# Weight sums formed at four places of a unit, operand blocks loaded a product sooner and split partly in the next unit

## The chip, the cores and the metric

The kernel runs on one core of a Trainium2 chip. Its time is the device time of one execution in microseconds (us). Engines are named as in the profile: PE multiplies matrices, PEld loads its weights, DVE works on vectors, ACT applies functions and copies, POOL is the third elementwise engine, and SP issues the DMA transfers from one queue, in order.

## The reference

One layer of a hybrid decoder is computed in float32 for a prompt of 2048 rows and for 8 sample rows. The dense products are what costs:

```python
h = rmsnorm(x, g_pre)
proj = h @ w_in                                  # 1024 x 10248: q,k | v | o | z_a | gates | u | v_b | z_b | gate_a | gate_b
hm = mlstm(silu(conv(q, k)), v, gates)           # 4 heads of 256, chunks of 128 rows
y_a = sigmoid(o) * rmsnorm(hm) * silu(z_a)
y_b = u * (tril(W_s) @ layernorm(v_b) + b) * silu(z_b)
merged = sigmoid(gate_a) * (y_a @ w_pa) + sigmoid(gate_b) * (y_b @ w_pb)
x = x + rmsnorm(merged @ w_out)
x = x + sigmoid(x @ w_ple_gate) * rmsnorm(p @ w_ple)
```

## The kernel before, in words

**Passes and units.** The prompt goes through in 4 passes of 512 rows (`p` 0 to 3). A pass is a chain of 28 units, each a product of a 512 x 1024 block of rows with 1024 x 512 columns of a weight: for each head h the units v, qk, og, gg, and then ub0 to ub3, pa0, pa1, pb0, pb1, wo0, wo1, wg0, wg1. Pass 1 also carries the sample rows.

**A unit is seven products.** A unit is a 2 x 2 block product by Strassen and Winograd (`run_unit`, table `ORDER`): with the weight blocks A11, A12, A21, A22 the weight sums S1 = A21+A22, S2 = S1−A11, S3 = A11−A21, S4 = A12−S2 are formed, and with the row blocks B the sums T1 to T4. The seven products are taken in the order A11·B11, A12·B21, S2·T2, S1·T1, S3·T3, S4·B22, A22·T4; unit wo0 has an order of its own (`LATE`: A11, S4, S2, S1, S3, A12, A22). They are called product 0 to product 6 here.

**Splitting.** Float32 operands are cut into a high and a low part, and each term is three matmuls (high·low, high·high, low·high). So every weight operand needs a high part (`whi`: ACT, L124) and a low part (`wlo`: DVE or, every fourth one in pass 0, POOL in two halves; L129), and so does every row operand (`rhi`, `rlo`). A product is 24 matmuls of 128 x 128 x 256 (L484 where rows are the moving side, L487 where weights are).

**The stream of weights.** `Stream` runs ahead of the products. At the start of product k `reach_high` cuts the high part of the weight that product k+2 will need and issues loads; half way through the product `reach_low` forms the low part and then the sums up to three products ahead (`SUM = 3`). Weight sums are only formed in pass 0. There A11, A21, A22 of a unit are fetched together, A11 first, and A12 after them. The sums are kept in DRAM: S3 whole, S1, S2, S4 as their parts; the later passes load them. In the kernel before, `sum` forms S1 (into a new tile `wsum`), S3 (into A21's tile) and S2 (into A11's tile) in one batch when S2's turn comes, which is in the last product of the unit before; S4 (into A12's tile) comes in product 2. For wo0 all four stand in one batch.

**Row operands of the next stage.** Units ub3, pa1 and wg1 carry a generator `ahead` that is stepped once after each product. `from_dram` (ub3 and pa1) loads four blocks `blk` of 512 KB each (`ya` or `yb`) and then runs `build`, which makes the seven split row operands B11, B21, T2, T1, T3, B22, T4 of the next stage, one a step; `hahead` (wg1) does so for the rows of the next pass. In the kernel before, the step after product 0 does nothing, the loads are issued after product 1, and what `build` has left is run at the unit's end.

**What sets the order.** A list scheduler places the instructions of each engine by the program's order and its own estimates. Every engine and the SP queue run in order. Buffers are pools that rotate: 13 weight tiles (`w`), 14 of row operands (`res`), 10 pieces (`p4`).

Of the kernel before, what the change touches and what calls it, by code (L numbers as in the profile page):

```python
# [74 lines left out]
def tile_layer(ctx: ExitStack, tc: tile.TileContext, I, O):  # L75
# [171 lines left out]
        S.activation(junk[0:rws, 0:n], x, AF.Square, scale=scale, accum_out=acc_out)  # L247


    class Stream:  # L250


# [41 lines left out]
            store(self.kept[u, n].rearrange("p (k c) -> p k c", k=4), t)  # L294

        def sum(self, p, u, n):
            first = "S4" if order(u) is LATE else "S2"
            if p or n not in (first, "S4"):
                return
            at = self.raw  # L300
            a11, a12, a21, a22 = (at[p, u, m] for m in RAW)
            if n == first:
                s1 = self.tile(u, "wsum")
                add(s1, a21, a22)
                self.keep(u, "S1", s1)
                sub(a21, a11, a21)
                self.keep(u, "S3", a21)
                sub(a11, s1, a11)
                self.keep(u, "S2", a11)
            if n == "S4":  # L310
                s4 = self.tile(u, "wsum") if first == "S4" else a12
                sub(s4, a12, at[p, u, "S2"])
                self.keep(u, "S4", s4)

        def reach_high(self, n):
            end = len(self.items)
# [124 lines left out]
                else:  # L441
                    add(dst(sel), ps[..., c], self.extra[:, sel, c])

    def run_unit(p, u, res, tok, consumer, slhs=None, ahead=None):
        w = width(u) if tok else res.w
        packed = w == 256
        accs, so = {}, None
# [17 lines left out]
        for wn, bn, an, opens in order(u):  # L465
# [50 lines left out]
                x2 = None  # L516
            if ahead is not None:
                next(ahead, None)
        for _ in ahead or ():
            pass  # L520


    class Box:
# [88 lines left out]

    def hahead(box):
        drain(qa)
        yield
        (b11, b12), (b21, b22) = box.blk
        yield from build(box.res, b11, b12, b21, b22)
# [346 lines left out]
    def v_unit(A, h):  # L964
        p, res = A.p, A.res
        vh, vl = (piece([P, NC, DV], F32R, nm) for nm in ("vh", "vl"))
        xh = piece([P, NC, 256], name="xh")
        if h == 0:
            A.gs = small([P, NC + 1, 8], "gs")
            if p == SP:  # L970
                G.memset(A.gs[:, NC, :], 0.0)

        def done(i, l, o):
            if i == "sample":
                sv = tiny([NS, DH], "sv")
                samp_sum(sv, l[0])
                store(svd[:, h * DH:(h + 1) * DH], sv)
                x = A.xs[h // 2][:, (h % 2) * 256:(h % 2 + 1) * 256]
                samp_sum(x, l[1])
                V.bn_stats(A.st[0:NS, NC, h, :], x)  # L980
                if h == 0:
                    samp_sum(A.gs[0:NS, NC, 0:4], l[0], 256, 4)
                    samp_sum(A.gs[0:NS, NC, 4:8], l[1], 256, 4)
                return
            sl = slice(2 * l, 2 * l + 2)
            if i == 0:
                if o.extra is None:
                    for sel, ps in o.parts:
                        split_to(vh[:, sl, :][:, sel, 0:DH], vl[:, sl, :][:, sel, 0:DH], ps[..., 0:DH], V)
                else:  # L990
                    t = tmp([P, 2, DH], "vt")
                    o.into(lambda sel: t[:, sel, :], 0, DH)
                    split_to(vh[:, sl, 0:DH], vl[:, sl, 0:DH], t, V)
            else:
                o.into(lambda sel: xh[:, sl, :][:, sel, :], 0, DH)
                for c in range(2 * l, 2 * l + 2):
                    V.bn_stats(A.st[:, c, h, :], xh[:, c, :])
            if h == 0:
                o.into(lambda sel: A.gs[:, sl, 4 * i:4 * i + 4][:, sel, :], 256, 260, V)

        run_unit(p, ("v", h), res, True, done, A.slhs)
        drain(qa)
        store(A.xhd[h].rearrange("p (c f) -> p c f", c=NC), xh)
        G.memset(vh[:, :, DH:DH + 1].bitcast(F32), 1.0)
        G.memset(vh[:, :, DH + 1:DV].bitcast(F32), 0.0)
        G.memset(vl[:, :, DH:DV].bitcast(F32), 0.0)
        if h == 0:
            n = NC + (1 if p == SP else 0)
            V.tensor_tensor(A.gs[:, 0:n, :], A.gs[:, 0:n, :], bg.unsqueeze(1).broadcast_to([P, n, 8]), op=ALU.add)
            qb.append(gates(p, A.gs, A.gt))  # L1010
        return vh, vl
# [18 lines left out]
    def branch(p, box, res):  # L1030
        A = BranchA()
        w = tw(p)
        A.p, A.res, A.gt = p, res, Box()
        A.slhs = box.slhs if p == SP else None
        A.xs = [tmp([NS, 512], "xs") for _ in range(2)] if p == SP else None
        A.st = small([P, NC + 1, 4, 6], "bst")
        A.xhd = [spill([P, NC * 256], f"xh{p}_{h}") for h in range(4)]
        A.sgd = [[spill([P, 4 * w], f"sg{p}_{i}{j}") for j in range(4)] for i in range(2)]
        A.yad = [[spill([P, 4, w], f"ya{p}_{kh}{l}") for l in range(2)] for kh in range(2)]
        A.ybd = [[spill([P, 4, w], f"yb{p}_{kh}{l}") for l in range(2)] for kh in range(2)]  # L1040
        st = None
        if p == SP:
            st = once([P, 16, NS, 3], "st")
        for h in range(H):
            v = v_unit(A, h)
            q, k = qk_unit(p, h, res)
            g = og_unit(p, h, res)
            while not hasattr(A.gt, "done"):
                advance(qb)
            qa.append(attention(h, p, q, k, g, v, A.gt, A.yad))  # L1050
            if p == 0 and h == 0:
                qb.append(consts_b())
            if p == SP and h == 0:
                qb.append(sample_conv_state(st))
            if p == SP:
                qb.append(sample_head(h, st, A.gt, A.yad))
            gg_unit(A, h)
        b_norm(A)
        A.ra = Res(w)
        for j in range(4):  # L1060
            ub_unit(A, j, from_dram(A.ra, A.yad) if j == 3 else None)
        return A

    def final_state():
# [180 lines left out]
    def ub_unit(A, j, ahead):  # L1245
# [42 lines left out]
                store(A.ybd[j // 2][l][:, 2 * (j % 2):2 * (j % 2) + 2, :], y[:, :, l, :])  # L1288
            yield

        run_unit(p, ("ub", j), A.res, False, done, ahead=ahead)
        qc.append(tail())


    def from_dram(res, d):
        yield
        drain(qa)
        drain(qb)
        b = [[piece([P, 4, res.w], name="blk") for _ in range(2)] for _ in range(2)]
        for kh in range(2):  # L1300
            for l in range(2):
                load(b[kh][l], d[kh][l])
        yield
        yield from build(res, b[0][0], b[0][1], b[1][0], b[1][1])

    def merge(A, pbox):
# [9 lines left out]
        for j in range(2):  # L1316
# [10 lines left out]

            if j:
                drain(qc)
            run_unit(p, ("pa", j), ra, False, done, ahead=from_dram(rb, A.ybd) if j else None)  # L1330
            ma[j] = sg
        qc.append(pprep(p, pbox))
        rm = Res(HT)
# [67 lines left out]
        for j in range(2):  # L1401
# [10 lines left out]
                    V.tensor_tensor(g, t, g, op=ALU.mult)  # L1412
                add(m, m, g, V if j else G)

            run_unit(p, ("pb", j), rb, False, done, ahead=ready(False) if j else None)
        return rm, lhs[0], ready(True)


# [84 lines left out]
    def out_phase(p, rm, slhs, late, pbox, box):  # L1503
# [138 lines left out]
        for d in range(2):  # L1642
# [29 lines left out]
                    store(O["y_prompt"][0, p * TP:(p + 1) * TP, 256 * nq:256 * nq + 256].rearrange(  # L1672
                        "(c q) f -> q c f", q=P), xq[nq])

            run_unit(p, ("wg", d), rx, True, done, slhs2, hahead(box) if d and p + 1 < NP else None)
        if p == SP:
            for i in range(2):
                store(O["y_sample"][:, 0, 512 * i:512 * i + 512], xs[i])


    box = Box()
    for i, _ in enumerate(hprep(0, box)):
        if i == 0:
            consts_vecs()
# [64 lines left out]
```

## Time and profile before

| | |
|---|---|
| median of 3 runs | 2907.65 us (2901.53 to 2907.81) |
| the profiled execution | 2909.96 us |
| its span, first to last instruction | 2908.3 us |
| mean granted clock of PE, of full speed | 0.972 |
| pass 0, 1, 2, 3 (from the trace) | 831.1, 756.3, 657.8, 656.8 us |

The span is what the trace covers; the 1.7 us around it belong to the execution. A busy time is that of one engine, a wait is idle time of an engine just before an instruction, put down to what came last. The pass limits are the starts of the passes' first products; the first product of all starts at 17.9 us.

### The profile page before, as it was taken

The numbers are of one execution on the slowest core, as the hardware profiler recorded it, in microseconds if no ns is written. First come the engines' busy times: TensorE is split into PE (matmuls) and PEld (weight loads), VectorE is DVE, ScalarE is ACT, GpSimd is POOL, SyncE is SP. The second block draws the span as 40 slices with busy tenths as digits, with TensorE's granted clock in tenths as the row PEclk, the third lists the DMA queues.
The fourth block names the chain that finished last, engine by engine and source line by source line (L and its number), as shares of the span: only waits on it lengthen the run. The fifth ranks groups of instructions, "written<-read, shape, count | busy, mean of one in ns | idle before, by whom it ended". The sixth has DMA issues, their size and how long they took to land. (4 is left out here: it accounts for less than half of the span.)

```text
span 2908.3 us, 56208 instructions
## 1 busy us (share of the span) xinstructions
PE 2712.1 (93%) x21835; PEld 2643.8 (91%) x21835; DVE 2207.6 (76%) x3645; ACT 1563.8 (54%) x2704; POOL 492.3 (17%) x557
## 2 busy tenths in 40 slices
PE   6999898887899999999989999999999999999898
PEld 6898898777889889989989999999898999999898
DVE  7898898798887767777778776665779776765777
ACT  4555556444646555454456555554456555554445
POOL 3323323233421100101011100001021100001010
PEclk8899999899999999999999999999999999999999
DMA  5575666775787878888877777778888877788886
GB/s 212 190 268 224 229 250 253 276 282 210 274 284 236 279 267 273 264 287 311 310 239 253 268 260 258 257 269 290 313 300 278 284 258 261 254 276 272 315 287 227
DMA packets 268628, 770.38 MB, mean 265 GB/s; under 512 B 30065, under 2 KB 89337, under 8 KB 268354
## 3 DMA queue, kind: packets, MB, share of 16 engines
q1 hardware_dynamic: 268362, 766.79, 75.5%
q8 instruction: 172, 2.82, 0.4%
q14 instruction: 94, 0.77, 0.1%
HBM read 595.29 MB, written 171.53 MB: 264 GB/s over the span
## 5 line engine op out<-in xcount | busy, mean ns | idle before, releaser
L487 PE MATMUL acc<-rhi,wlo 128*128 128x256 f32 (+1 forms) x4480 | 1277.0, 286 | 60.2 <-DVE wlo L129 47.0
L487 PE MATMUL acc<-rhi,whi 128*128 128x256 f32 (+1 forms) x4480 | 1291.5, 288 | 38.8 <-ACT whi L124 24.1
L487 PE MATMUL acc<-rlo,whi 128*128 128x256 f32 (+1 forms) x4480 | 1275.9, 285 | 0.0
L487 PEld LDWEIGHTS acc<-rhi,wlo 128*128 128x128 f32 x4480 | 859.8, 192 | 71.3 <-DVE wlo L129 56.0
L487 PEld LDWEIGHTS acc<-rhi,whi 128*128 128x128 f32 x4480 | 860.8, 192 | 51.4 <-ACT whi L124 28.0
L487 PEld LDWEIGHTS acc<-rlo,whi 128*128 128x128 f32 x4480 | 860.6, 192 | 0.0
L129 DVE TENSOR_TENSOR wlo<-wraw,whi 128x1024 fp32r<-128x1024 f32 (+1 forms) x461 | 588.5, 1280 | 163.4 <-PE acc L487 61.6
L124 ACT ACTIVATE whi<-wraw 128x1024 fp32r<-128x1024 f32 (+1 forms) x503 | 527.4, 1054 | 298.1 <-PE acc L487 88.4
L484 PE MATMUL acc<-whi,rhi 128*128 128x256 f32 (+1 forms) x1792 | 516.6, 289 | 22.8 <-ACT whi L124 7.8
L484 PE MATMUL acc<-wlo,rhi 128*128 128x256 f32 (+1 forms) x1792 | 511.9, 288 | 17.4 <-DVE wlo L129 13.9
L484 PE MATMUL acc<-whi,rlo 128*128 128x256 f32 (+1 forms) x1792 | 509.4, 285 | 9.0 <-DVE rlo L129 9.0
L484 PEld LDWEIGHTS acc<-whi,rhi 128*128 128x128 f32 x1792 | 345.7, 193 | 29.2 <-ACT whi L124 10.0
L484 PEld LDWEIGHTS acc<-wlo,rhi 128*128 128x128 f32 x1792 | 344.1, 193 | 22.4 <-DVE wlo L129 17.4
L484 PEld LDWEIGHTS acc<-whi,rlo 128*128 128x128 f32 x1792 | 345.5, 193 | 9.8 <-DVE rlo L129 9.7
L124 ACT ACTIVATE u<-acc 128x512 f32<-128x512 f32 (+1 forms) x272 | 140.4, 519 | 350.1 <-PE acc L487 281.8
L129 POOL TENSOR_TENSOR wlo<-wraw,whi 128x512 fp32r<-128x512 f32 x84 | 143.3, 1727 | 235.7 <-ACT whi L124 213.4
L139 DVE TENSOR_TENSOR u<-acc,u 128x512 f32<-128x512 f32 (+1 forms) x136 | 80.2, 593 | 77.7 <-PE acc L487 46.7
L124 ACT ACTIVATE s<-acc 128x512 f32<-128x512 f32 (+1 forms) x136 | 69.5, 517 | 93.8 <-PE acc L487 66.4
L1286 POOL TENSOR_TENSOR yb<-yb,ub 128x512 f32<-128x512 f32 (+1 forms) x32 | 48.9, 1536 | 303.9 <-DVE yb L1264 91.5
L786 POOL TENSOR_TENSOR so<-so,sz 128x512 f32<-128x512 f32 (+1 forms) x32 | 46.4, 1450 | 302.0 <-DVE sz L783 302.0
L241 POOL TENSOR_SCALAR aab<-au 128x2 f32<-128x2 f32 x32 | 7.8, 243 | 501.4 <-DVE au L879 475.5
L865 DVE SCALAR_TENSOR_TENSOR cext<-cext,fst,smp 128x258 f32<-128x258 f32 x128 | 60.5, 476 | 31.4 <-PE smp L802 31.0
(368 smaller groups left out, 3967.4 us busy)
## 6 DMA issues: line engine op xcount, KB each, us to landing
wraw<-in_w_main SPq DMA_DIRECT2D x351, 512.0 KB
xh<-xh SPq DMA_DIRECT2D x32, 512.0 KB
sg<-sgm SPq DMA_DIRECT2D x24, 512.0 KB
gsig<-sg SPq DMA_DIRECT2D x24, 512.0 KB
x<-in_x_prompt SPq DMA_DIRECT2D x16, 512.0 KB
ya<-ya SPq DMA_DIRECT2D x32, 256.0 KB
xr<-in_x_prompt SPq DMA_DIRECT2D x32, 256.0 KB
pg<-pg SPq DMA_DIRECT2D x32, 256.0 KB
```

The lines of the kernel that those rows point to most:

```text
L124: S.activation(out, in_, AF.Copy)
L129: eng.tensor_tensor(lo, full, hi.bitcast(F32), op=ALU.subtract)
L139: (eng or V).tensor_tensor(out, a, b, op=ALU.add)
L241: G.tensor_scalar(out, ms, EPS, None, op0=ALU.add)
L484: T.matmul(outs[s], x[:, kt, s * P:(s + 1) * P], wt[:, kt, :], start=first, stop=last, skip_group_check=not opens)
L487: T.matmul(outs[s], wt[:, kt, s * P:(s + 1) * P], x[:, kt, :], start=first, stop=last, skip_group_check=not opens)
L786: G.tensor_tensor(so[:, s], so[:, s], sz[:, s], op=ALU.mult)
L865: V.scalar_tensor_tensor(cext[:, h, kt, :], cext[:, h, kt, :], gt.fst[:, h, self.c:self.c + 1], p3, op0=ALU.mult, op1=ALU.add)
L1286: G.tensor_tensor(y[:, :, l, :], y[:, :, l, :], ub[:, :, l, :], op=ALU.mult)
```

## The change

The sums get a table of places: S3 is formed a product earlier than before (in product 5 of the unit before), S2 where the batch stood (product 6), S1 in product 0 of its own unit, S4 in product 2 as before. S3 is still A11−A21 in A21's tile; S2 becomes A22−S3 in the new tile `wsum`, and S1 becomes A11+S2 in A11's tile. The number of sums and of tiles is the same. For wo0 the sums come as S3, then S2 and S4, then S1.

`from_dram` issues its loads with the step after product 0 and steps `build` after products 2 to 6, as before; the last two operands, B22 and T4, are no longer run at the unit's end but handed on (`carry`) and stepped after products 0 and 1 of the next unit (pa0, pb0, and v0 of the next pass). `hahead` starts `build` one product later than before, and its last two operands go into the next pass.

```diff
+    SUMS = {1: ("S3",), 2: ("S2",), 3: ("S1",), 5: ("S4",)}
+    SUMS_LATE = {0: ("S3",), 1: ("S2", "S4"), 3: ("S1",)}
...
         def sum(self, p, u, n):
-            first = "S4" if order(u) is LATE else "S2"
-            if p or n not in (first, "S4"):
+            if p:
                 return
-            at = self.raw
-            a11, a12, a21, a22 = (at[p, u, m] for m in RAW)
-            if n == first:
-                s1 = self.tile(u, "wsum")
-                add(s1, a21, a22)
-                self.keep(u, "S1", s1)
-                sub(a21, a11, a21)
-                self.keep(u, "S3", a21)
-                sub(a11, s1, a11)
-                self.keep(u, "S2", a11)
-            if n == "S4":
-                s4 = self.tile(u, "wsum") if first == "S4" else a12
-                sub(s4, a12, at[p, u, "S2"])
-                self.keep(u, "S4", s4)
+            place = [m for m, *_ in order(u)].index(n)
+            at = {m: self.raw.get((p, u, m)) for m in RAW + ("S2", "S3")}
+            for m in sums_of(u).get(place, ()):
+                if m == "S3":
+                    t = at["A21"]
+                    sub(t, at["A11"], t)
+                elif m == "S2":
+                    t = self.tile(u, "wsum")
+                    sub(t, at["A22"], at["S3"])
+                elif m == "S1":
+                    t = at["A11"]
+                    add(t, t, at["S2"])
+                else:
+                    t = self.tile(u, "wsum") if order(u) is LATE else at["A12"]
+                    sub(t, at["A12"], at["S2"])
+                at[m] = t
+                self.keep(u, m, t)
...
-        for _ in ahead or ():
-            pass
+        if not carry:
+            for _ in ahead or ():
+                pass
...
     def hahead(box):
         drain(qa)
+        yield
         yield
...
     def from_dram(res, d):
-        yield
         drain(qa)
         drain(qb)
         b = [[piece([P, 4, res.w], name="blk") for _ in range(2)] for _ in range(2)]
         for kh in range(2):
             for l in range(2):
                 load(b[kh][l], d[kh][l])
+        yield
         yield
```

On DVE, at the change from unit og1 to gg1 in pass 0, the program before has these rows (`wsum<-wraw` is S1 of gg1, `wraw<-wraw` S3, `wraw<-wsum,wraw` S2, the `wraw<-wraw` at the end S4; `sz` belongs to og1):

```order
L129 TENSOR_TENSOR wlo<-wraw,whi 128x1024
L139 TENSOR_TENSOR wsum<-wraw 128x1024
L129 TENSOR_TENSOR ql<-q,qh 128x256
L136 TENSOR_TENSOR wraw<-wraw 128x1024
L783 SCALAR_TENSOR_TENSOR sz<-sz,vecs,szg 128x512
L136 TENSOR_TENSOR wraw<-wsum,wraw 128x1024
L783 SCALAR_TENSOR_TENSOR sz<-sz,vecs,szg 128x512
L129 TENSOR_TENSOR cl<-cext,ch 128x516
L136 TENSOR_TENSOR wraw<-wraw 128x1024
L139 TENSOR_TENSOR sgm<-acc,s_2520 128x2x256
```

The changed program has these at the same place (the first `wraw<-wraw` is S3, `wsum<-wraw` S2, `wraw<-wraw,wsum` S1):

```order
L136 TENSOR_TENSOR wraw<-wraw 128x1024
L739 SCALAR_TENSOR_TENSOR k<-k,sg 128x512
L139 TENSOR_TENSOR so<-acc,u_2328 128x2x256
L129 TENSOR_TENSOR wlo<-wraw,whi 128x1024
L136 TENSOR_TENSOR wsum<-wraw 128x1024
L794 SCALAR_TENSOR_TENSOR sz<-sz,vecs,szg 128x512
L139 TENSOR_TENSOR wraw<-wraw,wsum 128x1024
L794 SCALAR_TENSOR_TENSOR sz<-sz,vecs,szg 128x512
L129 TENSOR_TENSOR ql<-q,qh 128x256
L139 TENSOR_TENSOR sgm<-acc,s_2520 128x2x256
L129 TENSOR_TENSOR wlo<-wraw,whi 128x1024
```

S3 has gone up past a `wlo`, and S2 stands where S1 stood, as the first of the unit change instead of the third.

On POOL, at the same place, the program before has (`so<-so,sz` belongs to og1, `wlo<-wraw,whi` behind it is the low part of S2 of gg1, in two halves, and then that of another weight):

```order
L129 TENSOR_TENSOR wlo<-wraw,whi 128x512 x2
L786 TENSOR_TENSOR so<-so,sz 128x512 x2
L129 TENSOR_TENSOR wlo<-wraw,whi 128x512 x4
L1004 MEMSET vh 128x4
L1005 MEMSET vh 128x4
```

The changed program has (S2 now lies in `wsum`):

```order
L129 TENSOR_TENSOR wlo<-wraw,whi 128x512 x2
L797 TENSOR_TENSOR so<-so,sz 128x512
L129 TENSOR_TENSOR wlo<-wsum,whi 128x512 x2
L797 TENSOR_TENSOR so<-so,sz 128x512
L129 TENSOR_TENSOR wlo<-wraw,whi 128x512 x2
```

The low part of S2 has moved ahead of the second multiply; so it is in gg0, gg2 and gg3.

On ACT, in unit ub3 of pass 0, the program before has (`rhi<-blk` are the high parts of B11 and B21 of pa0, `u` a copy of a sum out of PSUM, `whi` the weights of ub3 and pa0):

```order
L124 ACTIVATE s_6387<-acc 128x512
L124 ACTIVATE whi<-wsum 128x1024
L124 ACTIVATE whi<-wraw 128x1024
L124 ACTIVATE u_6476<-acc 128x512
L124 ACTIVATE rhi<-blk 128x1024 x2
L124 ACTIVATE whi<-wraw 128x1024 x4
L124 ACTIVATE u_6558<-acc 128x512
```

The changed program has:

```order
L124 ACTIVATE s_6387<-acc 128x512
L1269 ACTIVATE xh<-xh,bnb,brs 128x256 x2
L124 ACTIVATE rhi<-blk 128x1024 x2
L124 ACTIVATE u_6476<-acc 128x512
L124 ACTIVATE whi<-wraw 128x1024 x4
L124 ACTIVATE u_6558<-acc 128x512
```

Both `rhi<-blk` now stand before `u`, and still ahead of the four `whi`.

## Rows read from the trace of the kernel before

**Rows 1.** Page: busy us, share of span and instructions of each engine.

```profile
PE 2712.1 (93%) x21835; PEld 2643.8 (91%) x21835; DVE 2207.6 (76%) x3645; ACT 1563.8 (54%) x2704; POOL 492.3 (17%) x557
```

**Rows 2.** Windows: length; busy PE, PEld, DVE, ACT, POOL (instructions); PE clock, DMA, GB/s.

```profile
0.00:831.10 831.10, 711.04 (x5401) 689.36 (x5402) 712.69 (x940) 457.02 (x725) 274.96 (x234) 0.93 0.66 244
...
1587.40:2245.20 657.80, 641.63 (x5327) 635.16 (x5326) 473.73 (x771) 359.24 (x614) 64.33 (x103) 0.99 0.80 278
147.40:253.30 105.90, 96.62 (x767) 94.65 (x766) 94.03 (x127) 61.10 (x95) 33.20 (x31) 0.95 0.64 241
546.00:636.70 90.70, 70.82 (x538) 68.70 (x538) 80.00 (x79) 42.68 (x51) 29.86 (x16) 0.89 0.77 284
...
559.50:572.70 13.20, 2.71 (x11) 2.35 (x11) 9.73 (x7) 5.25 (x6) 3.76 (x2) 0.58 0.90 349
```

**Rows 3.** Waits of PE in pass 0: total us, times, longest us.

```profile
PE acc L487 <- DVE wlo L129: 23.4, 18, 3.1
PE acc L487 <- ACT whi L124: 20.2, 10, 7.4
PE acc L487 <- POOL wlo L129: 13.0, 6, 3.8
...
PE acc L484 <- DVE wlo L129: 8.8, 5, 4.4
PE acc L484 <- DVE rlo L129: 8.6, 2, 6.5
...
PE acc L484 <- ACT rhi L124: 4.8, 2, 4.2
```

**Rows 4.** Groups of DVE in pass 0, by form: busy us, mean ns, idle before.

```profile
L136 DVE TENSOR_TENSOR wraw<-wraw 128x1024 f32<-128x1024 f32 x53 | 72.0, 1359 | 0.2
L136 DVE TENSOR_TENSOR wraw<-wsum,wraw 128x1024 f32<-128x1024 f32 x27 | 36.5, 1351 | 0.0
L139 DVE TENSOR_TENSOR wsum<-wraw 128x1024 f32<-128x1024 f32 x27 | 34.1, 1263 | 0.7 <-DMA wraw<-in_w_main 0.7
```

**Rows 5.** Timeline of the first product, DVE, then PE: start, us, instruction, [idle before].

```profile
18.60 1.23 DVE L139 TENSOR_TENSOR wsum<-wraw 128x1040 f32<-128x1040 f32 x1
...
22.10 1.23 DVE L136 TENSOR_TENSOR wraw<-wsum,wraw 128x1040 f32<-128x1040 f32 x1
...
23.85 1.21 DVE L129 TENSOR_TENSOR rlo<-hblk,rhi 128x1024 fp32r<-128x1024 f32 x1
...
25.12 0.59 PE L484 MATMUL acc<-whi,rlo 128*128 128x260 f32 x1 [6.47 <-DVE rlo L129]
```

**Rows 6.** Timeline of POOL in the first unit.

```profile
26.43 7.87 POOL L129 TENSOR_TENSOR wlo<-wsum,whi 128x520 fp32r<-128x520 f32 x2 [13.75 <-ACT whi L124]
```

**Rows 7.** Timeline of unit gg1, POOL, then PE.

```profile
225.37 2.22 POOL L786 TENSOR_TENSOR so<-so,sz 128x512 f32<-128x512 f32 x1 [10.36 <-DVE sz L783]
228.22 1.66 POOL L786 TENSOR_TENSOR so<-so,sz 128x512 f32<-128x512 f32 x1 [0.63 <-DVE sz L783]
229.84 4.47 POOL L129 TENSOR_TENSOR wlo<-wraw,whi 128x512 fp32r<-128x512 f32 x2
...
232.13 0.58 PE L487 MATMUL acc<-rhi,wlo 128*128 128x256 f32 x1 [3.79 <-POOL wlo L129]
```

**Rows 8.** Timeline of unit ub3 in pass 0: SP, ACT, PE.

```profile
555.83 4.18 SPq L117 DMA_DIRECT2D blk<-ya  x4
...
562.48 1.06 ACT L124 ACTIVATE rhi<-blk 128x1024 fp32r<-128x1024 f32 x1 [5.34 <-DMA blk<-ya]
...
566.99 0.58 PE L487 MATMUL acc<-rhi,whi 128*128 128x256 f32 x1 [7.42 <-ACT whi L124]
```

**Rows 9.** Tile blk, all passes: idle of its engine until its load landed (us, times).

```profile
  DMA blk<-ya: 16.6, 8
  DMA blk<-yb: 10.9, 6
```

**Rows 10.** Waits of ACT in pass 0, columns as in Rows 3.

```profile
ACT whi L124 <- DMA wraw<-in_w_main: 13.0, 10, 4.3
```

More of the change, by code (lines that the diff above doesn't have):

```diff
@@ L247, in sumsq, with sums_of @@
         S.activation(junk[0:rws, 0:n], x, AF.Square, scale=scale, accum_out=acc_out)
+    SUMS = {1: ("S3",), 2: ("S2",), 3: ("S1",), 5: ("S4",)}
+    SUMS_LATE = {0: ("S3",), 1: ("S2", "S4"), 3: ("S1",)}
+    def sums_of(u):
+        return SUMS_LATE if order(u) is LATE else SUMS
     class Stream:
@@ L442, in into, with run_unit @@
                     add(dst(sel), ps[..., c], self.extra[:, sel, c])
-    def run_unit(p, u, res, tok, consumer, slhs=None, ahead=None):
+    def run_unit(p, u, res, tok, consumer, slhs=None, ahead=None, carry=False):
         w = width(u) if tok else res.w
@@ L999, in done @@
                 o.into(lambda sel: A.gs[:, sl, 4 * i:4 * i + 4][:, sel, :], 256, 260, V)
-        run_unit(p, ("v", h), res, True, done, A.slhs)
+        run_unit(p, ("v", h), res, True, done, A.slhs, A.hahead if h == 0 else None)
         drain(qa)
@@ L1033, in branch @@
         A.p, A.res, A.gt = p, res, Box()
+        A.hahead = box.ahead
         A.slhs = box.slhs if p == SP else None
@@ L1060, in branch @@
         for j in range(4):
-            ub_unit(A, j, from_dram(A.ra, A.yad) if j == 3 else None)
+            if j == 3:
+                A.ahead = from_dram(A.ra, A.yad)
+            ub_unit(A, j, A.ahead if j == 3 else None)
         return A
@@ L1289, in tail @@
             yield
-        run_unit(p, ("ub", j), A.res, False, done, ahead=ahead)
+        run_unit(p, ("ub", j), A.res, False, done, ahead=ahead, carry=True)
         qc.append(tail())
     def from_dram(res, d):
-        yield
         drain(qa)
@@ L1329, in merge @@
                 drain(qc)
-            run_unit(p, ("pa", j), ra, False, done, ahead=from_dram(rb, A.ybd) if j else None)
+            if j:
+                A.ahead = from_dram(rb, A.ybd)
+            run_unit(p, ("pa", j), ra, False, done, ahead=A.ahead, carry=bool(j))
             ma[j] = sg
@@ L1413, in done @@
                 add(m, m, g, V if j else G)
-            run_unit(p, ("pb", j), rb, False, done, ahead=ready(False) if j else None)
+            run_unit(p, ("pb", j), rb, False, done, ahead=ready(False) if j else A.ahead)
         return rm, lhs[0], ready(True)
@@ L1673, in done @@
                         "(c q) f -> q c f", q=P), xq[nq])
-            run_unit(p, ("wg", d), rx, True, done, slhs2, hahead(box) if d and p + 1 < NP else None)
+            box.ahead = hahead(box) if d and p + 1 < NP else None
+            run_unit(p, ("wg", d), rx, True, done, slhs2, box.ahead, carry=True)
         if p == SP:
@@ L1681, in tile_layer @@
     box = Box()
+    box.ahead = None
     for i, _ in enumerate(hprep(0, box)):
```

## The prediction

> **What bounds the kernel now.** I read the page first: PE is busy 93% of the span, DVE 76%, ACT 54% [rows 1], so PE sets the time and only what makes PE wait, or run at its lower clock, can be won. The windows then show where that is. Pass 2 has PE idle for 657.80 − 641.63 = 16.2 us; pass 0 has it idle for 831.10 − 711.04 = 120.1 us, at a granted clock of 0.93 of full speed instead of 0.99, and DVE is busy there for 712.69 us, 86% [rows 2]. Pass 0 alone forms weight sums and splits every weight, so the part of the change that touches the sums plays in the 831 us of pass 0, and the reader should expect little from the other three. A head's four units in pass 0 take 105.90 us with DVE busy 94.03, 89% [rows 2]: PE is the bound on average, DVE is close behind.
>
> The waits of PE in pass 0 come third. Those on the weights' and rows' parts that are shown are 23.4 + 20.2 + 13.0 + 8.8 + 8.6 + 4.8 = 78.8 us [rows 3]. All have one form: a high or low part was not ready when its product's turn came. The mean of the largest group is 23.4/18 = 1.3 us, which is about the length of one DVE instruction of 128 x 1024 (1.26 to 1.36 us [rows 4]): PE waits for an operand that stands one or two places too far back in DVE's order.
>
> **The change part by part.** The count of sums is the same: 53 + 27 + 27 of them in the shown forms, 72.0 + 36.5 + 34.1 = 142.6 us of DVE in pass 0 [rows 4]. Nothing is saved in work; what moves is the order. A batch of three is 1.26 + 1.36 + 1.35 = 4.0 us of DVE at each unit change, spread by the change over three products, so that at most one sum stands ahead of a split at a time.
>
> *First product.* The three sums and three `hblk` steps lie between 18.60 and 23.85 ahead of the `rlo` that PE waits 6.47 us for [rows 5]. In the new order only S2 is left there: S3 is formed among the earlier steps, where the weights' landing and not DVE sets the pace, and S1 after the row splits. Two sums of 1.15 us spacing go, 2.3 us, and a little of the next wait (4.2, the longest of the group on `rhi` [rows 3]): the high part of S3 no longer stands ahead of T2's. −3, between −2.3 and −6.5.
>
> *S2 in the gate units.* POOL forms the low part of S2 behind two multiplies, 2.22 and 1.66 us; it starts at 229.84 and PE waits 3.79 us until 232.13 [rows 7]. Three of the six waits in this group are of that size (longest 3.8 [rows 3]), 11.4 us. The change takes the second multiply, 1.66 us, and its 0.6 us gap out of the way: −2.3 each, −7 in all; between 0 and −11.4. That the multiply then ends later costs nothing: its result is read by the attention's end, a unit on.
>
> Here a rule speaks against the gain. The row: two halves of 128 x 520 took POOL 7.87 us while DVE ran instruction after instruction, where the pair of 128 x 512 took 4.47 [rows 6, 7]. The Trainium skill, page "SBUF — State Buffer", section "SBUF: two separate sides", says that DVE (with two inputs in SBUF) and GpSimd share one port pair, that it is an exclusive lock for a whole instruction, and that the other fully blocks. By that rule a sum laid beside POOL's low part holds it up again, the three gate units give nothing, and the forecast would be 7 us higher; 7.87 us for one pair agrees with it, 4.47 only in part, so I keep −7.
>
> *Other waits on low parts from DVE.* 23.4 + 8.8 = 32.2 us in 23 waits [rows 3]. The longest of the second group, 4.4 us, is S4 of wo0 behind its batch of four; the new order puts S3 a product ahead and S1 two products behind: −3.5. Of the 23.4 I take half, −11.5: in the head units they sit at S3, whose sum now comes a product sooner, in pa and pb at S2, S3 and S4 behind a batch. The bounds are 0 (the waits are for DVE's sheer load) and −23.4.
>
> *Unit ub3 and the blocks.* The four loads were issued from 555.83 on, and the first landed at 562.48, where ACT had waited 5.34 us; four `whi` stood behind the two `rhi` on ACT's order, and PE waited 7.42 us for the first of them [rows 8]. The loads come a product sooner, which is at most 3.3 us (pass 2: 641.63 us of PE for 7 x 28 products and the small work between them [rows 2]); ACT was ready for them at 562.48 − 5.34 = 557.14, so of its wait some 2 us may stay. In SP's order they now also pass the two stores of S1's parts, which wait for DVE. −6.5, between −3 and −10 (with the wait on DVE that follows it). The copy `u` out of PSUM now stands behind both `rhi` on ACT; if a load is late, it and DVE's work on it wait too. Further waits on ACT's `whi` in pass 0: 20.2 − 7.4 = 12.8 us; I take −2.
>
> *Later passes.* ACT and DVE sat idle for 16.6 + 10.9 = 27.5 us until blocks landed, in 14 places [rows 9]; 5.3 are counted above. Of the other 22 PE can have felt at most what idle time its passes have, 16.2 us in pass 2. I take −5 for all three, between 0 and −15. B22 and T4, handed on, are two `rhi` and two `rlo` at each of eleven unit changes (two in each pass, and three between passes); they leave the end of one unit, where they came in a burst, for the start of the next, whose own products need them only as product 5 and 6. Cost nothing, covered by three products.
>
> *Clock.* After ub3's waits the granted clock was 0.58 in a window with 2.71 us of PE work [rows 2]; a stretch in which PE waits is followed by one at 1.2 instead of 2.4 GHz. Pass 0 stands at 0.93 against 0.99, some 0.06 x 711 = 43 us. With 33 of 120 us of idle time gone I let the same share of it go: −12, between 0 and −20.
>
> *Given back.* Without this a head loses 2.3 us at S2, some 3.5 at S3 and its other low parts, and 2 of the clock, 8 us; 94.03/(105.9 − 8) is 96% of DVE. The densest stretch shown is 89%, at which a head would win nothing (a rival, below), and short gaps in which DVE waits for PE or ACT will stay; since 89% was reached with DVE working ahead of need, I take 94%, at which a head takes 100.0 us, 2 us more. Over four heads +8, and +4 for the units after, of which ub3 to pa1 have DVE at 88% [rows 2]: +12, between 0 and +30.
>
> Sum: −3 −7 −3.5 −11.5 −6.5 −2 −5 −12 +12 = −38.5. From the profiled execution's 2909.96 us that is 2871.5; the median of the runs shown, 2907.65, is 2.3 lower, so I predict 2868 us (the sum less 2.3 is 2869; I leave a us for waits too small to be shown).
>
> **The rivals.**
>
> *DVE takes most of it back.* The waits leave their places and come again as DVE's load: a wait on a low part is then one for DVE to get through 94 of 106 us. For it: 89% in a head, 88% around ub3, a mean of 1.36 us for a sum, where a split of that size took 1.21 [rows 4, 5]. Against it: PE's waits are for single operands with DVE doing work that nobody needs yet. Only the places where no DVE load decides are won: first product 3, ub3 6.5, blocks 5, a third of the clock 4: 2907.65 − 18.5 = 2889.
>
> *Everything in pass 0 goes.* The 78.8 us fall to a fifth, −63, the clock gives −20, blocks −10, DVE gives back +12: 2907.65 − 81 = 2827. For it: one cause, the batch, is near most of these waits. Against it: DVE would be at 95% in pass 0 as a whole (712.69 of 750).
>
> *The change moves waits without removing any.* S3's low part was not late because of its sum but because of its place behind other splits, S2's low part on POOL waits again by the lock, and ub3's blocks land late beside a weight load: within 8 us of 2907, about 2903. For it: the number of instructions is unchanged and the DMA share around ub3 is 0.77 to 0.90 [rows 2]. Against it: two batches less at the first product and in wo0 are sure.
>
> *Slower.* S3's sum now needs A21 a product sooner, and DVE, in order, would stand still for it: behind it are the low parts of the running unit, and PE waits for them. In pass 0 ACT already waited ten times for a weight's landing, 13.0 us, longest 4.3 [rows 10], and A21 comes behind A11; DVE itself waited 0.7 us for a weight [rows 4]. If DVE's wait is 1.3 us (the mean of ACT's) at each of 27 unit changes, it is 35 us and takes the whole gain; at 2.8, half way to the longest, it is 76 us: 2868 + 76 = 2944. It decides from 1.4 us a unit. Against it: 0.7 us in two waits says that today the weights land well ahead of the sums in nearly every unit; a product is up to 3.3 us.
>
> **How the numbers follow.** Chances: forecast 0.55 (own range 2848 to 2884), DVE takes it back 0.21, everything goes 0.08, no change 0.09, slower 0.07. The range that should hold the time 8 times in 10 leaves out the slower case, half of the no-change case and the lower half of "everything goes": 2825 to 2903. A difference under 0.3%, 8.7 us, can't be told from none here. Faster: 0.55 + 0.21 + 0.08 = 0.84, less 0.01 for a weaker second case: 0.83. Same: 0.10. Slower: 0.07.
>
> **What would show it.** In the changed trace's pass 0: at the first product PE waits some 4 us instead of 6.5; in gg1 to gg3 POOL's low part follows the first multiply, PE waits 1.5 us there instead of 3.8; in ub3 ACT waits under 2 us for `blk` and PE's 7.42 is gone; PE's waits on DVE's `wlo` are about 20 us instead of 32; the clock of pass 0 is 0.94 or 0.95, its length near 800 us with DVE at 89 to 90%. The forecast is wrong if a head stays above 103 us (then DVE is the bound), if DVE waits for `wraw` from DRAM for more than some 10 us in pass 0 (the slower case), or if passes 1 to 3 move by more than 15 us.

## The result, and the profile after

The changed kernel took 2879.02 us (median of 4 runs, 2869.2 to 2882.19), the kernel before 2907.73 us (2901.53 to 2907.82): a ratio of 0.9901, 95% interval 0.9873 to 0.9928, or 28.7 us less. Forecast were 2868 us, 39.7 us less. The time lies in the stated range and in the forecast's own, 2848 to 2884 us; the forecast's ratio, 0.9863, lies just under the interval: the gain is there, and over a quarter smaller than forecast. That sum hides terms that missed in both directions; they are taken apart below.

The windows of the changed kernel, cut at its passes, at the second head and at ub3 to pa1 (columns as in [rows 2]):

```profile
0.00:808.30 808.30, 698.62 (x5401) 674.82 (x5402) 716.37 (x942) 456.19 (x724) 273.13 (x234) 0.94 0.69 251
808.30:1561.90 753.60, 724.14 (x5819) 690.88 (x5818) 559.21 (x1180) 405.27 (x784) 94.52 (x132) 0.99 0.80 274
1561.90:2215.50 653.60, 638.53 (x5327) 631.58 (x5326) 475.75 (x771) 359.27 (x614) 65.24 (x103) 0.99 0.80 280
2215.50:2869.00 653.50, 636.31 (x5289) 630.73 (x5288) 461.83 (x749) 342.80 (x583) 64.83 (x89) 0.99 0.78 271
145.90:246.40 100.50, 93.19 (x765) 90.79 (x765) 93.40 (x128) 61.34 (x97) 32.20 (x31) 1.00 0.67 254
523.60:614.00 90.40, 72.90 (x539) 70.82 (x538) 82.40 (x80) 42.49 (x51) 29.23 (x16) 0.87 0.79 286
```

Pass 0, counted from the span's start, went from 831.1 to 808.3 us (−22.8). The three later passes together, up to the end of the last product (in the changed kernel 1 us behind the last window of passes above), went from 2070.9 to 2061.7 us (−9.2). In pass 0 PE's idle time fell only from 120.1 [rows 2] to 808.30 − 698.62 = 109.7 us, −10.4; the other 12.4 us are PE's own busy time, 711.04 to 698.62 for the same 5401 matmuls: the granted clock. The second head shows it: 100.5 instead of 105.9 us, at clock 1.00 instead of 0.95, with DVE at 93.40/100.50 = 93%. The stretch from ub3 to pa1 has won nothing (90.40 against 90.70).

Within the heads the gain sits in the og units. Measured between the first products of the units, og0 to og3 took 89.5 instead of 104.9 us, while the four gate units went up from 128.2 to 131.2. In og1 to og3 DVE is busy for 99 to 100% of the time in both kernels; in gg1 to gg3 it was busy for 83 to 84% and is now for 95 to 97%. So DVE work went from units that were full of it to units that had room. gg0 alone lost 6.0 us (34.5 to 40.5): PE never waited in it before and now waits 3.4 us, and its busy time there rose from 34.5 to 37.1 us, at clock 0.83 instead of 0.85.

PE's waits in pass 0 of the changed kernel (total us, times, longest; answers to [rows 3]; L493 and L496 are the lines L484 and L487 of before):

```profile
PE acc L496 <- DVE wlo L129: 16.5, 16, 7.4
PE acc L493 <- DVE wlo L129: 11.8, 6, 4.4
PE acc L496 <- POOL wlo L129: 11.8, 7, 3.0
PE acc L496 <- ACT u L124: 11.1, 8, 2.8
PE acc L496 <- ACT whi L124: 11.0, 8, 3.4
...
PE acc L493 <- ACT whi L124: 7.9, 4, 3.9
...
PE acc L493 <- ACT rhi L124: 4.1, 2, 3.6
...
PE acc L493 <- DVE rlo L129: 2.9, 3, 2.1
```

The six groups of [rows 3] come to 58.1 us instead of 78.8, 20.7 less; PE's idle time fell by half of that, so that the rest came back under other names, among them ACT's copy `u` (11.1 us at L496, 7.4 before). Two things stand out. The largest group has a single wait of 7.4 us that was not there. And the waits on low parts at L493, the row units, rose from 8.8 to 11.8 us.

The first is ub3. DVE, ACT, POOL and PE there, in the changed kernel (answers to [rows 8]):

```profile
535.18 1.23 DVE L129 TENSOR_TENSOR rlo<-blk,rhi 128x1024 fp32r<-128x1024 f32 x1 [3.27 <-ACT rhi L124]
...
538.50 2.13 DVE L136 TENSOR_TENSOR blk<-blk 128x1024 f32<-128x1024 f32 x1
540.54 2.28 DVE L129 TENSOR_TENSOR rlo<-blk,rhi 128x1024 fp32r<-128x1024 f32 x1
...
544.95 3.42 DVE L129 TENSOR_TENSOR wlo<-wraw,whi 128x1024 fp32r<-128x1024 f32 x2
```

```profile
534.09 1.06 ACT L124 ACTIVATE rhi<-blk 128x1024 fp32r<-128x1024 f32 x1 [1.64 <-DMA blk<-ya]
536.90 1.06 ACT L124 ACTIVATE rhi<-blk 128x1024 fp32r<-128x1024 f32 x1 [1.75 <-DMA blk<-ya]
...
538.34 1.05 ACT L124 ACTIVATE whi<-wraw 128x1024 fp32r<-128x1024 f32 x1
```

```profile
538.26 3.48 POOL L1300 TENSOR_TENSOR yb<-yb,ub 128x512 f32<-128x512 f32 x2 [9.36 <-DVE yb L1278]
542.51 3.64 POOL L129 TENSOR_TENSOR wlo<-wraw,whi 128x512 fp32r<-128x512 f32 x2 [0.77 <-DMA S1l_ub<-wlo]
```

```profile
547.29 0.58 PE L496 MATMUL acc<-rhi,wlo 128*128 128x256 f32 x1 [7.41 <-DVE wlo L129]
```

ACT's wait for the first block went as forecast (5.34 to 1.64; it now waits 1.75 for the second as well), and the wait of 7.42 us on ACT is gone. But S3's low part stands on DVE behind two splits and two sums of the blocks, and two of these take 2.13 and 2.28 us where the first `rlo` took 1.23: POOL works on 128 x 512 tiles at the same time. This is the port pair of DVE and GpSimd that the Trainium skill describes (page "SBUF — State Buffer", section "SBUF: two separate sides"); the trace agrees, in that the slow ones are those beside POOL (538.26 to 541.74).

The second is in wo1, where DVE forms S3 of the next unit, wg0 (DVE, then PE):

```profile
719.39 1.23 DVE L136 TENSOR_TENSOR wraw<-wraw 128x1024 f32<-128x1024 f32 x1 [9.80 <-DMA wraw<-in_w_main]
720.53 1.22 DVE L129 TENSOR_TENSOR wlo<-wraw,whi 128x1024 fp32r<-128x1024 f32 x1
```

```profile
721.81 0.58 PE L493 MATMUL acc<-wlo,rhi 128*128 128x256 f32 x1 [4.36 <-DVE wlo L129]
```

DVE stood still for 9.80 us at S3's sum of wg0, because A21 had not landed, and the low part that PE waited for stood behind it. This is the mechanism that the prediction's slower rival named. The groups of DVE in pass 0 (columns as in [rows 4]) give its size, and the price of all sums:

```profile
L136 DVE TENSOR_TENSOR wraw<-wraw 128x1024 f32<-128x1024 f32 x27 | 40.3, 1493 | 21.8 <-DMA wraw<-in_w_main 21.8
L136 DVE TENSOR_TENSOR wsum<-wraw 128x1024 f32<-128x1024 f32 x27 | 38.3, 1418 | 0.2 <-PE acc L496 0.2
L136 DVE TENSOR_TENSOR wraw<-wraw,wsum 128x1024 f32<-128x1024 f32 x26 | 36.9, 1420 | 0.0
L139 DVE TENSOR_TENSOR wraw<-wraw,wsum 128x1024 f32<-128x1024 f32 x27 | 36.5, 1350 | 0.1
```

It came in five units: ub1, ub2, pa0, pb0 and wo1, each time for the unit that follows. The sums themselves now take 152.0 instead of 142.6 us [rows 4] for the same 107, since more of them lie beside POOL's work: with wo0's S4 counted in, 51 of 108 instead of 34. Those took 1.65 and 1.59 us on average; a sum with nothing on POOL beside it took at most 1.23 us in either trace.

### The profile page after: what moved, and what is told of

The parts are those of the page before. It is cut to its first block, busy times and chain, and to the rows that moved or that the text cites. A ratio compares the mean times of both kernels' runs of the same rounds, so it can differ in the third digit from the quotient of the medians.

```text
span 2876.2 us, 56228 instructions
## 1 busy us (share of the span) xinstructions
PE 2698.6 (94%) x21835; PEld 2628.8 (91%) x21835; DVE 2216.2 (77%) x3645; ACT 1564.5 (54%) x2704; POOL 497.7 (17%) x557
## 3 DMA queue, kind: packets, MB, share of 16 engines
q1 hardware_dynamic: 268362, 766.79, 76.1%
## 5 line engine op out<-in xcount | busy, mean ns | idle before, releaser
L496 PE MATMUL acc<-rhi,wlo 128*128 128x256 f32 (+1 forms) x4480 | 1272.7, 285 | 44.9 <-DVE wlo L129 32.4
L496 PE MATMUL acc<-rhi,whi 128*128 128x256 f32 (+1 forms) x4480 | 1283.1, 287 | 32.5 <-ACT u L124 16.0
L496 PE MATMUL acc<-rlo,whi 128*128 128x256 f32 (+1 forms) x4480 | 1268.9, 283 | 0.0
L496 PEld LDWEIGHTS acc<-rhi,wlo 128*128 128x128 f32 x4480 | 853.1, 191 | 57.2 <-DVE wlo L129 42.0
L496 PEld LDWEIGHTS acc<-rhi,whi 128*128 128x128 f32 x4480 | 853.2, 190 | 43.2 <-ACT u L124 19.1
L496 PEld LDWEIGHTS acc<-rlo,whi 128*128 128x128 f32 x4480 | 853.4, 190 | 0.0
L493 PE MATMUL acc<-whi,rhi 128*128 128x256 f32 (+1 forms) x1792 | 516.1, 289 | 20.0 <-ACT whi L124 9.8
L493 PE MATMUL acc<-wlo,rhi 128*128 128x256 f32 (+1 forms) x1792 | 511.9, 287 | 19.9 <-DVE wlo L129 16.3
L493 PE MATMUL acc<-whi,rlo 128*128 128x256 f32 (+1 forms) x1792 | 510.1, 285 | 3.3 <-DVE rlo L129 3.3
L493 PEld LDWEIGHTS acc<-whi,rhi 128*128 128x128 f32 x1792 | 345.6, 193 | 25.6 <-ACT whi L124 11.2
L493 PEld LDWEIGHTS acc<-wlo,rhi 128*128 128x128 f32 x1792 | 344.1, 193 | 25.1 <-DVE wlo L129 20.3
L493 PEld LDWEIGHTS acc<-whi,rlo 128*128 128x128 f32 x1792 | 345.6, 193 | 4.2 <-DVE rlo L129 4.2
L129 POOL TENSOR_TENSOR wlo<-wraw,whi 128x512 fp32r<-128x512 f32 (+1 forms) x84 | 142.9, 1722 | 303.2 <-ACT whi L124 257.8
L1300 POOL TENSOR_TENSOR yb<-yb,ub 128x512 f32<-128x512 f32 (+1 forms) x32 | 55.3, 1739 | 297.8 <-DVE yb L1278 102.6
```

Source lines behind the costliest of these rows:

```text
L129: eng.tensor_tensor(lo, full, hi.bitcast(F32), op=ALU.subtract)
L493: T.matmul(outs[s], x[:, kt, s * P:(s + 1) * P], wt[:, kt, :], start=first, stop=last, skip_group_check=not opens)
L496: T.matmul(outs[s], wt[:, kt, s * P:(s + 1) * P], x[:, kt, :], start=first, stop=last, skip_group_check=not opens)
L1300: G.tensor_tensor(y[:, :, l, :], y[:, :, l, :], ub[:, :, l, :], op=ALU.mult)
```

## The experiments

The times are medians; the kernel before stood at 2906.4 to 2907.8 us beside them. The runs of one kernel spread over 7 to 19 us, and the interval of a ratio is 6 to 16 us wide, so that differences of a few us can't be read from medians. They are read from stretches of the profiles, of which there is one for each kernel, and those have noise too. In the four heads DVE, ACT and POOL run the same instructions in the same order in the kernel before and in `e2_blocks`: 447.0 and 441.9 us. They do so again in the changed kernel and in six of the runs below (e1_sums, e3_wg0, e3b_wg0, e6_nocarry, e9_early, e10_both): 428.5 to 434.2 us. So a single profile of the heads is good to some 5 us. Edits are shown in short form.

**The two parts alone.** `e1_sums` has the new places of the sums in the kernel before, `e2_blocks` the earlier loads and the carried splits. Each is half of the diff above.

```diff
 e1_sums:   + SUMS, SUMS_LATE, sums_of, sum()        (from_dram, hahead, carry as before)
 e2_blocks: + from_dram, hahead, carry, A.ahead ...  (sum() as before)
```

> The kernel before with the sums' new places alone (blocks and carry as before). Theory: the heads and ub0 to ub2 of pass 0 carry the gain, since there the changed kernel is 22 us shorter, and the sums alone touch them: 2907.7 - 20 = 2888 us, passes 1 to 3 within 2 us of before, and in unit ub3 of pass 0 the wait of 7.4 us on ACT's whi as before. Rival (the two parts need each other, DVE's load decides): under 8 us of gain, 2900 us or more.

> The kernel before with the blocks' earlier loads and the carried splits alone (sums as before). Theory: passes 1 to 3 get the 9 us that they lost in the changed kernel, pass 0 stays within 4 us, because in ub3 the wait only goes from ACT to DVE: 2898 us. Rival (the blocks won in ub3 of pass 0 too, and the sums' side took it back): 2890 us or less.

Measured: 2894.39 us for the sums alone (ratio 0.9944, 0.9926 to 0.9963), 2890.24 us for the blocks alone (0.9940, 0.9921 to 0.9959). The two gains, 13.4 and 17.5 us, add up to 30.9 against 28.7 together: within the noise the parts add up, and the blocks are about as much of the gain as the sums, while the forecast gave them 11.5 us (ub3 6.5, later passes 5). In the profile of e1_sums pass 0 is 14.4 us shorter, passes 1 to 3 are as before within 2 us, and ub3 still has a wait of 6.35 us on ACT's `whi`, as its theory said; its time lies between theory and rival. In that of e2_blocks the later passes won 8.9 us and pass 0 10.3 us, with ub3 at 31.5 instead of 35.8 us. So the blocks' earlier load does win in ub3 while the sums stand as before; together with the new sums ub3 is at 35.5 again (33.7 to 35.0 in e3_wg0, e3b_wg0, e4_poolgg and e6_nocarry below, which load the blocks at the same place). That is what the rival of the second expectation says; the time is at its bound of 2890.

**wg0's S3.** First S3 of wg0 was asked for a product later; then wg0 got the old batch.

```diff
 e3_wg0:  + SUMS_WG0 = {2: ("S3", "S2"), 3: ("S1",), 5: ("S4",)}      # wg0 only
 e3b_wg0: + if u == ("wg", 0) and place != 5:  S1, S3, S2 in one batch at place 2, as before
```

> The changed kernel with S3 of unit wg0 alone formed a product later (as before). Theory: DVE stood still for 9.8 us for that unit's A21, and PE waited 4.4 us behind it: that wait goes, 2879 - 5 = 2874 us. Rival (PE's wait there comes from the load of the other engines and only changes its name): 2879 us.

> The changed kernel, but unit wg0 of pass 0 forms its sums as before (S1 from A21 and A22 first, then S3 and S2, in one batch); the earlier try left S3's sum where it was in DVE's order, here it stands behind the low parts of wo1. Theory: DVE no longer stands still for 9.8 us for wg0's A21, PE's wait of 4.4 to 4.8 us in wo1 goes: unit wo1 of pass 0 43 instead of 47.8 us, 2880 - 5 = 2875 us. Rival (the wait moves on into wg0): wo1 and wg0 together 77 us as now, 2880 us.

e3_wg0 took 2880.7 us (0.9905, 0.9883 to 0.9926) and tested nothing: the scheduler put the sum at the same place on DVE, which stood still for 9.77 us as before. In e3b_wg0 the sum stands behind the low parts; DVE's standstill and PE's wait on S4's low part in wo1 are gone. But a wait of 3.75 us stands in the same unit instead, at a place where the kernel before, with the same batch, waits 5.11 us for the same `u`:

```profile
721.04 0.39 PE L504 MATMUL acc<-whi,rhi 128*128 128x256 f32 x1 [3.75 <-ACT u L124]
```

wo1 fell from 47.8 to 45.6 us and wg0 rose from 29.8 to 31.9: 77.5 us together, 77.6 in the changed kernel (76.1 in the kernel before: 42.7 and 33.4). In this profile wg1 is 2.9 us shorter; the time, 2882.86 us (0.9904, 0.9881 to 0.9926), does not show it and is the changed kernel's. The rival was right: the wait moves on into wg0.

**POOL in the gate units.**

```diff
+ if key[0] == 0 and key[1][0] == "gg" and key[2] in ("S2", "S1"):
+     pool = key[2] == "S1"
```

> The changed kernel, but in the four gg units of pass 0 POOL makes the low part of S1 instead of that of S2, and DVE that of S2. Theory: the four waits of 2.2 to 3.0 us at S2 come from POOL's multiply standing ahead of the low part, and go: 2879 - 9 = 2870 us. Rival (DVE's load decides: its 1.2 us more ahead of S2 and POOL's slow halves at S1 give the same waits at S1 and S3): 2877 to 2882 us.

Measured: 2883.14 us (0.9904, 0.9885 to 0.9924). The waits on POOL are gone, and others stand in their place (PE in pass 0; L498 is the product's line, L815 a matmul of the attention):

```profile
PE acc L498 <- DVE wlo L129: 21.3, 20, 7.9
...
PE smp L815 <- ACT kwh L126: 6.8, 3, 2.6
...
PE acc L498 <- POOL wlo L129: 0.3, 1, 0.3
```

11.8 − 0.3 = 11.5 us won on POOL, 21.3 − 16.5 = 4.8 lost on DVE's low parts and 6.8 on an operand of the attention, which waits for DVE in its turn. The four gg units take 131.9 instead of 131.2 us. The time is 1 us over the rival's range: nothing was won, as the rival says.

**How much slack DVE has.** One more instruction of 128 x 1024 a unit, in the changed kernel and in the kernel before, and one less in the heads of the changed kernel. In e12_less S4's product is that of the unchanged A12.

```diff
 e7_extra, e11_extra: + sub(S2, A22, S3)      # again, behind S4's sum; nobody reads it
 e12_less:            - sub(S4, A12, S2)      # in v, qk, og, gg of pass 0
```

> The changed kernel with one more DVE instruction of 128 x 1024 for each unit of pass 0 (S2's sum is formed a second time behind S4's, nothing waits for it): 28 x 1.25 = 35 us of DVE. Theory (PE waits for the place of an operand in DVE's order, DVE itself has slack): under 12 us more, 2880 to 2892 us. Rival (DVE's load is the bound of pass 0 by now): 25 to 35 us more, 2905 to 2915 us.

> The kernel before (sums in a batch, blocks late) with one more DVE instruction of 128 x 1024 behind S4's sum in each unit of pass 0 but wo0: 27 x 1.25 = 34 us of DVE. Theory (the batch left DVE slack that the new places used up): under 15 us more, 2907 + 11 = 2918 us, against 23 us in the changed kernel. Rival (DVE was the bound of the heads before as well): 20 us more or over, 2928 us.

> The changed kernel without S4's sum in the 16 head units of pass 0 (A12 is split in its place, so S4's product is another one): 16 x 1.4 = 22 us of DVE less in the heads. Theory by now (DVE's load is the bound of the heads, as one more instruction a unit cost 16 us of its 20 there): 12 to 18 us less in the heads, 2879 - 15 = 2864 us. Rival (the place of an operand in DVE's order decides): under 6 us less, 2873 us or more.

With one more instruction a unit the changed kernel went to 2902.33 us (0.9975 of the kernel before, 0.9963 to 0.9987), 23.3 us more for 35 us of DVE; the kernel before to 2923.19 us (1.0064, 1.0049 to 1.0079), 16.5 us more for 34. The four heads of the two (windows from the first product to ub0's):

```profile
18.90:463.50 444.60, 397.04 (x3050) 383.86 (x3049) 403.42 (x562) 248.23 (x377) 143.06 (x124) 0.94 0.62 230
```

```profile
17.90:472.20 454.30, 399.65 (x3050) 386.86 (x3049) 408.14 (x564) 248.87 (x379) 154.89 (x128) 0.93 0.60 225
```

Without it the heads were 428.6 us (DVE 389.3) in the changed kernel and 447.0 us (DVE 392.4) in the kernel before. There 15.8 us of DVE cost 7.3 us; in the changed one 14.1 us of DVE cost 16.0. That looks like some slack on DVE before and none after, but it is not shown. Set against the other profiles with the same order in the heads, the cost is 7 to 12 us before and 10 to 16 after, which overlap. By the ratios the whole programs lost 0.64% and 0.74%, 18.6 and 21.5 us, and the intervals overlap too. And the instruction did not come alone: the scheduler moved others with it, so that of the heads' DVE instructions 52 of 546 (before) and 83 of 544 (after) no longer stand in the old order. By the whole time neither expectation was met: 23.3 us lies just under the rival's 25, 16.5 between 15 and 20. What holds for both kernels is that an instruction that nobody waits for cost about half of its length or more in these runs, which speaks for PE waiting for DVE's load as well as for places in its order.

e12_less should have shown it from the other side, and did not: 2888.40 us (0.9936, 0.9920 to 0.9952), 9 us slower with less work. With S4's sum gone the scheduler moved S3's sum up on DVE, ahead of the attention's small steps, and in gg1 ahead of A21's landing:

```profile
223.07 1.72 DVE L129 TENSOR_TENSOR wlo<-wraw,whi 128x1024 fp32r<-128x1024 f32 x1
232.56 1.72 DVE L136 TENSOR_TENSOR wraw<-wraw 128x1024 f32<-128x1024 f32 x1 [7.77 <-DMA wraw<-in_w_main]
```

In gg1, gg2 and gg3 DVE stood still for 7.8, 7.9 and 8.9 us, and these units took 35.7, 36.1 and 36.3 us instead of 29.5, 31.7 and 29.5: 17.4 us for 24.6 us of standstill. The v and qk units, where DVE did not stand still for a weight, had 11.6 us less of DVE work and won 5.5 us, half of it. What the heads would take with less DVE work in the same order stays open; what a late weight costs is shown.

**The blocks sooner, and without the carry.**

```diff
 e9_early:   + ub2 steps the generator after its last product (loads), one empty step more before build
 e6_nocarry: + for _ in ahead or (): pass       # at the end of every unit, as before
```

> The changed kernel with the four ya blocks loaded a further product sooner, in ub2's last product, and the splits at the same products as now. Theory: in ub3 DVE is held in order by blocks that land late, and S3's low part stands behind it; the loads pass the stores of S2 in SP's order and come about 6 us sooner, so PE's wait of 7.4 us in ub3 of pass 0 falls under 3 us, ub3 from 35.5 to about 31 us, the later passes gain 1 to 2 us each: 2880 - 8 = 2872 us. Rival (DVE's load and POOL beside it decide in ub3): the wait stays at 6 us or more, 2878 to 2882 us.

> The changed kernel with the loads as early as there, but B22 and T4 run at the unit's end again, as before. Theory: the burst of two ACT and two DVE splits at eleven unit ends costs about half a microsecond each: 2880 + 6 = 2886 us. Rival (carrying is worth nothing, the earlier load is all): 2878 to 2882 us. Second rival (the carried splits hold up the next unit): 2874 us.

e9_early took 2873.50 us (0.9871, 0.9847 to 0.9895). ub3 fell from 35.5 to 31.7 us as expected (30.5 to 31.7 in the three runs with this load, 33.7 to 35.5 in the changed kernel and the four runs named above), but not for the reason given: in ub3 of pass 0 ACT no longer waits for a block at all, and PE still waits

```profile
547.55 0.58 PE L496 MATMUL acc<-rhi,wlo 128*128 128x256 f32 x1 [5.67 <-DVE wlo L129]
```

Its DVE is never idle in the 14 us before that, again with splits of 2.3 us beside POOL. So the landing was some 2 us of the changed kernel's 7.41 us, and the waits of 1.07 and 0.44 us on ACT ahead of it, which are gone too; DVE's own work is the rest. e6_nocarry took 2878.31 us (0.9900, 0.9877 to 0.9923): handing on B22 and T4 is worth nothing that can be measured, and the earlier load is what the blocks' part wins.

**Trying for more.**

```diff
 e10_both: e9_early + e3b_wg0
 e14_load: e9_early, and in reach_high  - else 5   + else 6
```

> The ya blocks another product sooner (e9_early) together with wg0's sums in one batch as before (e3b_wg0). Theory: the two places have nothing to do with each other; the 4 to 6 us that each saved in its profile add up: 2873.5 - 5 = 2868 us. Rival (wg0's wait goes on into wg0 and wg1): 2873 us.

> The kernel with the ya blocks another product sooner (e9_early), and in pass 0 the weights' loads a product sooner as well (6 places ahead instead of 5), so that A11, A21 and A22 of the next unit pass the two stores of S1 in SP's order. Theory: DVE stood still for 21.8 us in pass 0 ahead of S3's sums because A21 had not landed; that idle time falls under 5 us, wo1's wait of 4.4 us on S4's low part goes, 2873.5 - 6 = 2867 us. Rival (13 weight buffers are all taken, so that the loads wait for a buffer and not for their place): DVE's idle time stays over 15 us, 2872 to 2880 us, or slower where the loads now hold up the stores behind them.

e10_both took 2873.59 us (0.9889, 0.9873 to 0.9904), e9_early's time; the rival holds. e14_load took 2909.00 us (1.0006, 0.9996 to 1.0017), 35 us slower than e9_early. DVE's standstill ahead of the sums did not shrink (its wait in pass 0):

```profile
DVE wraw L136 <- DMA wraw<-in_w_main: 23.1, 7, 4.9
```

The earlier loads drew S3's sums forward with them, to product 3 in gg1 to gg3, where DVE waits again, 4.2 to 4.7 us each, and those units take 37 to 38 us. Whether buffers or the DMA queue hold the loads there, and why the heads lost 23 us in all, stays open. The fastest version is e9_early; its runs (2865.34 to 2875.48) overlap those of the changed kernel, and so does its interval, so that it is not shown to be faster than the changed kernel.

## Why the prediction was right, and where its terms were wrong

**Bound and direction.** Pass 0's order around the sums, with PE waiting for single operands, was the right place: e1_sums wins there and nowhere else. That DVE is close behind was right and too mild: the 89% of a head is a mean of units from 78% (qk) to 100% (og). The forecast took 33.5 us of idle time out of pass 0 and gave 12 back; PE's idle time fell by 10.4. That the time still lies within the forecast's own range is in part luck: the later passes gave 4 us more than their term, and the clock's term came out to the us.

**First product, −3: about −0.5.** The wait of 6.47 us [rows 5] became 3.57 us for a `rhi` that ACT now cuts behind S2's high part, and 0.29 for the `rlo`: 3.9 us, as forecast, and the next wait, 4.2 us on `rhi`, is gone. But at product 3 PE now waits 3.88 us for S1, whose sum had moved behind the row splits, and 1.79 for its low part on POOL; v0 took 36.5 instead of 37.0 us:

```profile
23.14 0.59 PE L493 MATMUL acc<-whi,rhi 128*128 128x260 f32 x1 [3.57 <-ACT rhi L124]
24.02 0.59 PE L493 MATMUL acc<-whi,rlo 128*128 128x260 f32 x1 [0.29 <-DVE rlo L129]
...
38.78 0.59 PE L493 MATMUL acc<-whi,rhi 128*128 128x260 f32 x1 [3.88 <-ACT whi L124]
```

The step asked what leaves DVE's queue ahead of the `rlo`, not who waits for the sum that was put off.

**S2 in the gate units, −7: about −1.** POOL does the low part behind one multiply instead of two, as the order said, and PE waits 2.6 to 3.0 instead of 3.8 us in gg1 to gg3: 3.1 us less in all, between the 7 of the sum and the nothing that the prediction sets against it. But gg0 has a new wait of 2.2, and the group as a whole fell only from 13.0 to 11.8. The step left out gg0, where no wait stood before, and where the unit lost 6.0 us. Why PE still waits over 2.6 us in the others, where 1.5 were forecast, was not settled; in gg1 the multiply that is left took 2.13 us and the two halves 3.15.

**Other low parts, −15: −12 and −0.** Leave out ub3 and the waits of 4.4 us in wo0 and wo1 on both sides, and 24.8 us of before are 12.2 after: the half that I took. With them the waits on DVE's low parts fell only from 32.2 to 28.3 us, where about 20 was the sign to look for. The −3.5 in wo0 was wrong: the wait is 4.35 us in both. In front of S4's low part stand the small splits of the unit's own row operands, not the batch. The further −2 on ACT's `whi` came out (12.8 to 11.0 at L496).

**ub3, −6.5: −0.3 in this profile.** The step that failed is the price of the wait that follows: PE's 7.42 us on ACT were taken to go but for a rest of ACT's own wait, and DVE's two splits and two sums of the blocks, which stand ahead of S3's low part, were not counted as what PE would wait for next. It waits 7.41 us for them.

**Later passes, −5: −9.2.** A bound of 15 was right and the value low; e1_sums shows that it is all the blocks'.

**Clock, −12, and given back, +12.** PE's busy time fell by 12.4 us. The 0.58 that the term starts from is the clock of a stretch with the waits in it; right behind, where PE was busy throughout, it was 0.91 (columns as in [rows 2]):

```profile
572.70:586.40 13.70, 13.70 (x110) 13.70 (x109) 11.97 (x14) 6.96 (x10) 0.00 (x0) 0.91 0.49 168
```

A head came to 100.5, 101.6 and 99.7 us (the second to the fourth), forecast was 100.0 at 94% of DVE; the second is at 93%. That DVE would now set the heads was put at 0.21 as a rival and at +12 in the sum. In og1 to og3, where DVE is busy without a gap, that is what the trace shows, before the change as after it; for the heads as a whole e7_extra and e11_extra leave it open.

**The slower rival** was given 0.07 as a whole and came true in five units, 21.8 us of DVE. I had written that over 10 us of it would prove the forecast wrong; it cost PE less than DVE, at least in wo1, where e3b_wg0 took 9.8 us of it away and won nothing in the median; what the other four standstills cost was not measured. What spoke against it, DVE's 0.7 us of before [rows 4], told only that no sum came too early then, not by how much: a sum that moves ahead needs the margin of its worst unit.

## What to carry to other kernels

When a batch is spread over an in-order engine, list what each moved piece now stands in front of and what it now waits for, on the other engines as well: in ub3, in wo1 and in the gate units of e4_poolgg a wait that went came back under the name of another operand or engine. Read an engine's load unit by unit: the mean of a head hid that its og units were full of DVE work and its gate units were not. Adding an instruction that nobody waits for is a cheap test of slack, but where a scheduler places the instructions it moves others too, and one profile each, good to 5 us here, did not tell 7.3 us from 16.0. Taking work out is not the mirror of it where a scheduler fills the hole: less work, and an operand asked for before its load, made the kernel 9 us slower.

## What was not expected of the hardware

In this pair of profiles the granted clock gave as much as the waits themselves: PE's idle time in pass 0 fell by 10.4 us, its busy time for the same matmuls by 12.4 us, and the second head, with fewer waits, ran at 1.00 instead of 0.95. How the gain is shared between the two changes from trace to trace: pass 0 of e9_early has PE idle for 102.5 us and busy for 703.2, that of e6_nocarry 111.8 and 696.3. The same 107 sums took 152.0 us when spread and 142.6 us in a batch, 9.4 us more of DVE, and the longer ones are those with POOL at work beside them.
